# Three-block fp32 kernel on Trainium2: two heads or four matrices in one inverse chain, with shared reciprocal roots

## The chip, the cores and the metric

The kernel runs on one core of one Trainium2 chip. The metric is the time of one execution on the device, in microseconds (us). The engines are TensorE (PE in the profile; PEld is its weight load), VectorE (DVE), ScalarE (ACT), GpSimd (POOL) and SyncE (SP), which issues the DMAs. Each engine executes its instructions in the order in which they were written into its queue.

## The reference

The reference runs three layers, one after the other, on x of 1 x 256 x 2048, all in fp32. The first has two kinds of heads, eight of each. The gated delta rule (GDN) heads need the inverse of a unit triangular matrix, the stick-breaking (SB) heads do not:

```python
# first layer, GDN heads (q, k after a causal convolution, SiLU and L2 norm)
lower = jnp.where(tri_strict, jnp.einsum('nbhik,nbhjk->nbhij', k_beta, k) * decay, 0.0)
t_inv = lax.linalg.triangular_solve(eye + lower, jnp.broadcast_to(eye, lower.shape),
                                    left_side=True, lower=True)
u = t_inv @ v_beta
w = t_inv @ (k_beta * jnp.exp(g)[..., None])
...
# first layer, SB heads (q, k after an RMS norm)
z = jnp.einsum('bhqd,bhkd->bhqk', q_blk, kh) * scale
log_stay = jnp.where(mask, jax.nn.log_sigmoid(-z), 0.0)
between = lax.cumsum(log_stay, axis=3, reverse=True) - log_stay
a = jnp.where(mask, jnp.exp(jax.nn.log_sigmoid(z) + between), 0.0)
...
# second layer, RWKV heads, run forward and backward in time
def step(S, inp):
    r_t, d_t, k_t, v_t, kk_t, b_t = inp
    sa = jnp.einsum('bhij,bhj->bhi', S, -kk_t)
    S = S * d_t[:, :, None, :] + sa[..., None] * b_t[:, :, None, :] + v_t[..., None] * k_t[:, :, None, :]
    return S, jnp.einsum('bhij,bhj->bhi', S, r_t)
```

The rest of the three layers is large projections and feed-forward products. The kernel does the second layer's scan in chunks of 128 rows, which again needs triangular inverses.

## The kernel before

All 256 rows are kept on the chip and the weights stream through it. A panel of weights comes by DMA into one of three slots (`wraw`); ScalarE casts it to its rounded part `whi` (L290), VectorE subtracts to get the rest `wlo` (L291), and TensorE multiplies the split rows with both (L309/L313, L335/L339, L369/L370/L374). A queue of `ada` steps (L496, a 128x2048 multiply with an accumulated sum, which makes the first layer's modulation) is spread over VectorE between the heads by `ada_some`.

Block 1 (to 1440 us) begins with a phase that loads x and the memory and projects the first rows (`project_rows`, to about 205 us). `block1_mix` then runs a loop of nine turns (about 205 to 600 us): GDN head h (`gdn_head`), SB head h-1 (`sb_head`), and the gate and split of GDN head h. Then come the output projection and the feed-forward part. Block 2 runs from about 1470 us with six calls of `rwkv_pair` (two heads, two directions, two chunks of 128 rows each), block 3 from about 2390 us.

`gdn_head` makes three convolved projections, the sums of squares and a reciprocal root on VectorE (`rsqrt`, 11 small operations, L399 to L413), the matrix `gnt` (L781), then calls `pair_inverse`. `rwkv_gram` makes the masked products (`gram`) of one chunk for two heads and calls `pair_inverse` for these two; so each `rwkv_pair` has two chains, one for each chunk. `pair_inverse` doubles the size of the inverted blocks six times. It keeps both the lower (`ylo`) and the upper, transposed inverse (`yup`). Level 0 puts single elements under a mask into both; a level l >= 1 is

- a product of the matrix and `ylo` (L1349),
- copies of `yup` to `z` and of the product to `t` on ScalarE (L1351, L1352),
- the two products `t` with `z` and `z` with `t` (L1358, L1359),
- masked puts of both results into `ylo` and `yup` on VectorE (L1339, `copy_predicated`).

The order on each engine is written by a scheduler that takes the program's order as priority and fills in other work where an instruction is not ready by its own reckoning; so the panels' products stand between the steps of the inverse. Buffers of a tag rotate (`tmp`, lanes A, B and S; two PSUM banks a lane for small products, two for `acc`). The level mask `lev` (128x896, loaded as 448 KB in fp32 and cast on VectorE at L242) is loaded once in the early phase and kept.

## Time and profile before

| | |
|---|---|
| runs, us | 3605.9, 3600.6, 3599.87 (median 3600.6) |
| profiled execution, us | 3601.28, its span 3599.5 |
| mean granted TensorE clock | 0.993 of full |
| busy: TensorE / VectorE / ScalarE / GpSimd | 3514.4 / 2662.4 / 1814.2 / 61.6 us |
| moved by DMA | 700.99 MB, mean 195 GB/s |

Busy times are shares of one span and say nothing of which engine waits for which. Matmul ends in the profile are modelled, so that a TensorE that is marked busy may be between two products. The granted clock is 1.00 at 2.4 GHz and 0.50 at 1.2 GHz; a figure between is a mean over a stretch that had both. The rows that matter stand in the section after the change.

### The profile page before, as it was taken

Reading aid. Unit: us, or ns where it says so; the run is one execution under the profiler, and the core shown is the slowest. Engines: PE = TensorE matmul, PEld = TensorE weight load, DVE = VectorE, ACT = ScalarE, POOL = GpSimd, SP = SyncE. Lnnn points to the kernel's source line nnn. Section 1 sums busy time; section 2 is a strip of 40 time slices with the busy share of each in tenths; the row PEclk is TensorE's granted clock in tenths of the full one; section 3 lists DMA queues with packets and bytes.
Section 4 is the critical chain, followed back from the end, with each engine's and each line's share of the span. In section 5 each row is a group of like instructions: output and inputs, shape, how many; then the busy total and the mean of one; then the engine's idle time right before and its main releaser. Section 6 shows DMA issues by size and latency. Waiting matters only on the chain.

```text
span 3599.5 us, 59008 instructions
## 1 busy us (share of the span) xinstructions
PE 3514.4 (98%) x22656; PEld 3144.6 (87%) x22656; DVE 2662.4 (74%) x5500; ACT 1814.2 (50%) x3138; POOL 61.6 (2%) x190
## 2 busy tenths in 40 slices
PE   8889999999999999999999999999999999999998
PEld 6889998999999998888888888889888888888887
DVE  7788988776767668877878867778776666666666
ACT  4156665544545455555555545554444544444444
POOL 0000000000000000000000000000000000000000
PEclk9989999999999999999999999999999999999999
DMA  8965777656666557332234336574445545555554
GB/s 337 351 237 200 263 266 265 225 208 219 222 206 231 188 181 239 133 125 107 103 115 138 125 117 213 188 253 170 172 168 185 187 176 202 176 198 180 195 184 144
DMA packets 128011, 700.99 MB, mean 195 GB/s; under 512 B 14449, under 2 KB 39537, under 8 KB 58865
## 3 DMA queue, kind: packets, MB, share of 16 engines
q1 hardware_dynamic: 127730, 697.22, 55.0%
q8 instruction: 179, 2.93, 0.3%
q14 instruction: 102, 0.84, 0.1%
HBM read 686.94 MB, written 10.22 MB: 194 GB/s over the span
## 4 chain that ended last, share of the span: by engine, by line
PE 86%; DVE 8%; ACT 3%; DMA 1%; issue 1%; SPq 0%; ACTq 0%; DVEq 0%
PE acc L335 36%; PE acc L339 18%; PE acc L309 12%; PE acc L313 6%; DVE wlo L291 2%; DVE ada L496 2%; PE acc L1349 1%; ACT whi L290 1%; PE acc L1358 1%; PE acc L1359 1%; PE acc L623 1%; PE acc L990 1%; PE acc L374 1%; DMA ada<-in_w_ada 1%; PE acc L369 1%
## 5 line engine op out<-in xcount | busy, mean ns | idle before, releaser
L290 ACT CAST whi<-wraw 128x1024 fp32r<-128x1024 f32 x1118 | 1096.1, 982 | 1199.0 <-PE acc L335 706.9
L291 DVE TENSOR_TENSOR wlo<-wraw,whi 128x1024 fp32r<-128x1024 f32 x1118 | 1272.7, 1140 | 514.5 <-ACT whi L290 412.4
L335 PE MATMUL acc<-a,whi 128*128 128x512 f32 x5888 | 1535.6, 396 | 6.7 <-ACT gt L346 1.7
L335 PEld LDWEIGHTS acc<-a,whi 128*128 128x128 f32 x5888 | 1043.1, 188 | 197.9 <-issue 5.4
L339 PEld LDWEIGHTS acc<-a,wlo 128*128 128x128 f32 x5888 | 816.9, 188 | 75.4 <-issue 4.0
L339 PE MATMUL acc<-a,wlo 128*128 128x256 f32 x5888 | 848.7, 282 | 0.0
L309 PE MATMUL acc<-a,whi 128*128 128x258 f32 (+1 forms) x3872 | 523.5, 284 | 0.2 <-ACT whi L290 0.2
L309 PEld LDWEIGHTS acc<-a,whi 128*128 128x128 f32 x3872 | 485.4, 190 | 0.9 <-ACT whi L290 0.4
L313 PE MATMUL acc<-a,wlo 128*128 128x258 f32 (+1 forms) x1936 | 282.8, 284 | 0.0
L313 PEld LDWEIGHTS acc<-a,wlo 128*128 128x128 f32 x1936 | 252.2, 190 | 0.3 <-issue 0.3
L496 DVE SCALAR_TENSOR_TENSOR ada<-ada,csilu 128x2048 f32<-128x2048 f32 x96 | 219.4, 2285 | 9.0 <-DMA ada<-in_w_ada 8.7
L1339 DVE COPY_PREDICATED ylo<-m_lev,acc 128x128 f32<-128x128 uint8 x200 | 82.8, 416 | 48.6 <-PE acc L1359 47.6
L369 PE MATMUL acc<-whi,a 128*128 128x256 f32 x416 | 108.3, 290 | 1.8 <-ACT whi L290 1.8
L1351 ACT COPY z<-yup 128x128 f32<-128x128 f32 x192 | 56.1, 300 | 102.5 <-DVE yup L1339 59.9
L370 PE MATMUL acc<-whi,a 128*128 128x256 f32 x416 | 107.6, 288 | 0.0
L356 DVE TENSOR_TENSOR x<-acc,x 128x256 f32<-128x256 f32 x128 | 54.2, 424 | 51.7 <-PE acc L339 51.7
L347 DVE TENSOR_TENSOR gt<-acc,gt 128x256 f32<-128x256 f32 x214 | 89.0, 418 | 3.5 <-ACT gt L346 2.9
L346 ACT COPY gt<-acc 128x256 f32<-128x256 f32 x214 | 78.0, 364 | 17.6 <-PE acc L339 17.6
L369 PEld LDWEIGHTS acc<-whi,a 128*128 128x128 f32 x416 | 80.0, 192 | 2.8 <-ACT whi L290 2.0
L370 PEld LDWEIGHTS acc<-whi,a 128*128 128x128 f32 x416 | 79.9, 192 | 0.0
L1359 PE MATMUL acc<-z,t 128*128 128x128 f32 x384 | 72.4, 278 | 0.2 <-ACT t L1352 0.2
L1358 PE MATMUL acc<-t,z 128*128 128x128 f32 x336 | 69.2, 290 | 2.0 <-ACT t L1352 2.0
(514 smaller groups left out, 3372.7 us busy)
## 6 DMA issues: line engine op xcount, KB each, us to landing
wraw<-in_w_up SPq DMA_DIRECT2D x132, 1024.0 KB, 4.8
ada<-in_w_ada SPq DMA_DIRECT2D x96, 1024.0 KB, 5.2
wraw<-in_w_down SPq DMA_DIRECT2D x128, 704.0 KB, 4.1
wraw<-in_w_out SPq DMA_DIRECT2D x48, 1024.0 KB, 4.9
wraw<-in_w_mg SPq DMA_DIRECT2D x48, 1024.0 KB, 4.9
wraw<-in_w_gate SPq DMA_DIRECT2D x44, 1024.0 KB, 4.7
wraw<-in_w_rs SPq DMA_DIRECT2D x20, 1024.0 KB, 5.1
wrow<-in_w_rows SPq DMA_DIRECT2D x16, 1024.0 KB, 8.5
```

Of the source, the lines that this page charges most:

```text
L290: nc.scalar.copy(hi[:, :m], raw[:, a:a + m])
L291: nc.vector.tensor_sub(lo[:, :m], raw[:, a:a + m], hi[:, :m].bitcast(F32))
L309: nc.tensor.matmul(acc, w, m, start=(n == 0), stop=False)
L313: nc.tensor.matmul(acc, lo[:, k % 8 * P:k % 8 * P + P], hs[k - c * kt][0], start=False, stop=(n == last))
L335: nc.tensor.matmul(both, hi[:, k % 8 * P:k % 8 * P + P], hs[k - c * kt][2], start=(n == 0), stop=False)
L339: nc.tensor.matmul(acc[:, :T], lo[:, k % 8 * P:k % 8 * P + P], hs[k - c * kt][0], start=False, stop=(n == last))
L347: self.nc.vector.tensor_add(out, acc[0], out)
L369: self.nc.tensor.matmul(accs[t], hs[k][0][:, ts], hi[:, ws], start=(k == 0), stop=False)
L370: self.nc.tensor.matmul(accs[t], hs[k][1][:, ts], hi[:, ws], start=False, stop=False)
L496: nc.vector.scalar_tensor_tensor(raw, raw, 1.0, self.cs, op0=ALU.mult, op1=ALU.mult, accum_out=self.mod[:, n:n + 1])
L1358: nc.tensor.matmul(pu4[:, 0, h], z2[:, h], t1[:, h], start=True, stop=True)
L1359: nc.tensor.matmul(pu4[:, 1, h], t1[:, h], z2[:, h], start=True, stop=True)
```

## The change

`gdn_head` becomes `gdn_pair`: the convolutions of two heads (lanes A and B), one reciprocal root for the eight columns of both, the preparation of both (`gdn_prep`), one `group_inverse` for the two matrices, both scans (`gdn_scan`), one reciprocal root for the four output columns. `sb_head` becomes `sb_pair`: the projections of two SB heads, one root of eight columns, then the two attends (`sb_attend`). The loop of `block1_mix` has five turns. In block 2, `rwkv_gram` no longer inverts: both chunks write into one tile `grams` (matrices of 128x512 in all), cleared by one memset on GpSimd, and one `group_inverse` takes the four matrices. In `group_inverse` a level makes all lower products and one put of all, then all upper products and one put of all. The level mask is loaded twice, in block 1's pool with two casts and in block 2's with four. In all, VectorE has 4969 instructions where it had 5406, ScalarE 2900 for 3092, GpSimd 156 for 194, TensorE 21043 as before.

```diff
-                self.load_mask(self.const, "lev")
...
+        self.lev2 = self.load_levels(bp, 2)
...
-        for h in range(9):
-            if h < 8:
-                with self.on("AB"[h % 2]):
-                    o = self.gdn_head(h)
-            if h:
-                self.sb_head(h - 1, ob)
-            if h < 8:
-                oa[h] = self.gdn_out(h, o, self.z_gate(h))
+        for i in range(5):
+            if i < 4:
+                pair = self.gdn_pair(2 * i)
+            if i:
+                self.sb_pair(2 * i - 2, ob)
+            if i < 4:
+                for h, o in enumerate(pair):
+                    oa[2 * i + h] = self.gdn_out(2 * i + h, o, self.z_gate(2 * i + h))
...
+    def gdn_pair(self, h0):
...
+        for j, lane in lanes:
+            with self.on(lane):
+                k = self.conv_proj("w1_k", h0 + j, 8 + h0 + j, "gk")
+                q = self.conv_proj("w1_q", h0 + j, h0 + j, "gq")
+                self.sumsq_cols(k, ss, 4 * j)
+                self.sumsq_cols(q, ss, 4 * j + 2)
+                kqv.append((k, q, self.conv_proj("w1_v", h0 + j, 16 + h0 + j, "gv")))
+        with self.on("A"):
+            nc.vector.tensor_scalar(sse, ss[:, :8], 1e-6, None, op0=ALU.add)
+            self.rsqrt(r, sse, [P, 8], "g")
+        preps = []
+        for j, lane in lanes:
+            with self.on(lane):
+                preps.append(self.gdn_prep(h0 + j, *kqv[j], r[:, 4 * j:4 * j + 4], sse[:, 4 * j:4 * j + 4], nt[:, j]))
+        lo, up = self.group_inverse(nt, self.lev2, "AB", lower=True)
+        outs = []
+        for j, lane in lanes:
+            with self.on(lane):
+                outs.append(self.gdn_scan(kqv[j][0], preps[j], [up[:, 1, j], lo[:, 1, j]]))
...
+    def sb_pair(self, h0, ob):
...
+        self.rsqrt(rk, mk, [P, 8], "s")
+        for j in range(2):
+            hv = slice(j * P, j * P + P)
+            self.sb_attend(h0 + j, *qk[j], rk[:, 4 * j:4 * j + 4], sv[0][:, hv], sv[1][:, hv], ob)
...
+        grams = self.bp.tile([P, 7, 4, P], F32, name=self.uid("gram"), tag="gram", bufs=1)
+        nc.gpsimd.memset(grams, 0.0)
         for n in range(2):
             with self.on("AB"[n]):
-                g, up = self.rwkv_gram(n, preps)
-                grams.append(g)
-                ups.append(up)
+                self.rwkv_gram(n, preps, grams)
+        _, up = self.group_inverse(grams[:, 0], self.lev4, "AB")
...
-        for h in range(H):
-            put(up, h, 0, mats[h])
-            put(lo, h, 0, pn[:, h * P:h * P + P])
+        put(up, 0, one(mats))
+        put(lo, 0, pn)
         for l in range(1, 7):
...
+            pt = bank(lanes[1])
+            for h, hc in enumerate(heads):
+                nc.tensor.matmul(flat(pt[:, hc], l), mats[:, h], zipped(lo, l, h, 1), start=True, stop=True)
+            nc.scalar.copy(flat(one(z2), l), zipped(up, l))
+            nc.scalar.copy(one(t1), pt)
             both = l < 6 or lower
+            pl = bank(lanes[0]) if both else None
+            if both:
+                for h, hc in enumerate(heads):
+                    nc.tensor.matmul(pl[:, hc], z2[:, h], t1[:, h], start=True, stop=True)
+                put(lo, l, pl)
+            pu = bank(lanes[1])
+            for h, hc in enumerate(heads):
+                nc.tensor.matmul(pu[:, hc], t1[:, h], z2[:, h], start=True, stop=True)
+            put(up, l, pu)
```

Where the order moves, three places. First VectorE at the start of block 1's heads, from the first sums of squares (`gss`) to the first puts of level 1; `ada` is a step of the modulation, `gnt` the matrix to be inverted, the last figures are the shape of the output. Before:

```order
L743 TENSOR_SCALAR gss_1465<-acc_1456 128x4
...
L779 SCALAR_TENSOR_TENSOR gdec_1492<-acc_1506,gnlam_1483,gdec_1492 128x128 x2
...
L781 TENSOR_TENSOR gnt_1511<-gdec_1492 128x128
...
L1339 COPY_PREDICATED yup_1528<-m_lev,gnt_1511 128x64x2
L1339 COPY_PREDICATED ylo_1527<-m_lev,acc_1533 128x64x2
...
L1339 COPY_PREDICATED ylo_1527<-m_lev,acc_1541 128x32x2x2
L1339 COPY_PREDICATED yup_1528<-m_lev,acc_1541 128x32x2x2
```

and now, from the first `ada` step behind a row copy on:

```order
L496 SCALAR_TENSOR_TENSOR ada_1783,mod<-ada_1783,csilu 128x2048
...
L1357 CAST m_lev_1403<-mraw_1404 128x7x128
...
L1357 CAST m_lev_1403<-mraw_1404 128x7x128
...
L748 TENSOR_SCALAR gss_1434<-acc_1433 128x8
...
L496 SCALAR_TENSOR_TENSOR ada_1852,mod<-ada_1852,csilu 128x2048
...
L821 SCALAR_TENSOR_TENSOR gdec_1529<-acc_1543,gnlam_1520,gdec_1529 128x128 x2
...
L822 TENSOR_TENSOR gnt_1436<-gdec_1529 128x128
L821 SCALAR_TENSOR_TENSOR gdec_1575<-acc_1589,gnlam_1566,gdec_1575 128x128 x2
...
L822 TENSOR_TENSOR gnt_1436<-gdec_1575 128x128
...
L1379 COPY_PREDICATED yup_1610<-m_lev_1403,gnt_1436 128x128x2
L1379 COPY_PREDICATED ylo_1609<-m_lev_1403,acc_1615 128x128x2
```

Both matrices `gnt` stand ahead of the first put (L1379), and two `ada` steps and the two casts of the mask have come ahead of it.

Second TensorE at the end of block 1's heads. L883/L917 spread the roots, L891/L925 make the scores, L906/L940 begin the sums over the softplus `ssp`, L915/L947 the output of an SB head; only products of the output panels stand in the places left out, and in the first gap before also the last GDN head. Before:

```order
L891 MATMUL acc_5967<-sq_q_5873,sq_k_5937 128x128 x3
...
L906 MATMUL acc_5980<-ssp_5972,c_negtri 128x128
...
L915 MATMUL acc_5987<-sz_5971,sv_5801 128x128
...
L883 MATMUL acc_6214<-c_ident,srk_6200 128x128 x2
L891 MATMUL acc_6218<-sq_q_6124,sq_k_6188 128x128 x3
...
L906 MATMUL acc_6231<-ssp_6223,c_negtri 128x128
...
L915 MATMUL acc_6238<-sz_6222,sv_5801 128x128
```

and now:

```order
L925 MATMUL acc_5829<-sq_q_5600,sq_k_5664 128x128 x3
...
L940 MATMUL acc_5842<-ssp_5834,c_negtri 128x128
...
L947 MATMUL acc_5849<-sz_5833,sv_5527 128x128
...
L917 MATMUL acc_5855<-c_ident,srk_5811 128x128 x2
L925 MATMUL acc_5859<-sq_q_5736,sq_k_5800 128x128 x3
...
L940 MATMUL acc_5872<-ssp_5864,c_negtri 128x128
...
L947 MATMUL acc_5879<-sz_5863,sv_5527 128x128
```

The scores of the last head now follow directly on the output of the one before it; 15 panel products (3.48 us of TensorE by the order's sizes at 0.23 us for 512 columns) stand between the scores and the sums of the first of the two heads, 4 (0.92 us) in the second.

Third TensorE inside an inverse of block 2: `gram` is the matrix, L1349/L1390 open a level, L335/L339 are products of the panels. Before (two chains, of buffers `ylo_20178` and `ylo_20301`):

```order
L335 MATMUL acc_20502<-a_15656,whi_20498 128x512
L1358 MATMUL acc_20227<-t_3520_20180,z_3521_20181 128x128
L1359 MATMUL acc_20227<-z_3521_20181,t_3520_20180 128x128
...
L1349 MATMUL acc_20314<-ylo_20301,gram_20279 128x128
...
L1349 MATMUL acc_20236<-ylo_20178,gram_20154 128x128
L1358 MATMUL acc_20320<-t_3543_20303,z_3544_20304 128x128
L1349 MATMUL acc_20236<-ylo_20178,gram_20156 128x128
L1359 MATMUL acc_20320<-z_3544_20304,t_3543_20303 128x128
...
L1358 MATMUL acc_20242<-t_3520_20180,z_3521_20181 128x128
...
L1349 MATMUL acc_20329<-ylo_20301,gram_20277 128x128
```

and now, from the last transpose on:

```order
L1384 MATMUL acc_19601<-c_ident,gram_19553 128x128
...
L335 MATMUL acc_19818<-a_15309,whi_19814 128x512
L1390 MATMUL acc_19608<-ylo_19595,gram_19553 128x128 x4
L335 MATMUL acc_19818<-a_15312,whi_19814 128x512
...
L1397 MATMUL acc_19615<-t_3383_19597,z_3384_19598 128x128 x4
L1401 MATMUL acc_19621<-z_3384_19598,t_3383_19597 128x128 x4
L1390 MATMUL acc_19627<-ylo_19595,gram_19553 128x128 x4
L339 MATMUL acc_19818<-a_15300,wlo_19815 128x256
...
L1397 MATMUL acc_19634<-t_3383_19597,z_3384_19598 128x128 x4
```

Four products stand together at each step of one chain, where the steps of two chains of two alternated.

## Rows read from the trace of the kernel before

**Rows 1.** The page's first part: busy us (share of the span) and instructions of each engine.

```profile
PE 3514.4 (98%) x22656; PEld 3144.6 (87%) x22656; DVE 2662.4 (74%) x5500; ACT 1814.2 (50%) x3138; POOL 61.6 (2%) x190
```

**Rows 2.** Busy time by stretch: us, each engine (instructions), granted clock, DMA share, GB/s.

```profile
205.00:240.00 35.00, 30.86 (x196) 28.26 (x196) 28.93 (x92) 22.80 (x54) 2.75 (x7) 0.80 0.49 161
...
260.00:575.00 315.00, 304.02 (x2452) 292.30 (x2451) 283.85 (x722) 197.86 (x450) 13.76 (x18) 0.99 0.70 249
575.00:605.00 30.00, 23.42 (x133) 19.24 (x132) 23.98 (x67) 20.39 (x47) 0.00 (x0) 0.94 0.55 200
...
1470.00:2140.00 670.00, 657.44 (x4095) 554.18 (x4094) 533.22 (x1499) 354.65 (x798) 32.13 (x78) 1.00 0.33 114
```

**Rows 3.** Groups by line, TensorE, 260-575 us: count | busy, mean | idle before.

```profile
L1358 PE MATMUL acc<-t,z 128*128 128x128 f32 x84 | 18.6, 303 | 1.6 <-ACT t L1352 1.6
L1349 PE MATMUL acc<-ylo,gnt 128*128 128x128 f32 x84 | 18.0, 295 | 3.4 <-DVE ylo L1339 1.1 <-DVE rs L400 1.0 <-ACT go L841 0.6
...
L1342 PE MATMUL acc<-c_ident,gnt 128*128 128x128 f32 x7 | 2.0, 292 | 1.8 <-DVE gnt L781 1.8
```

**Rows 4.** The same view of TensorE, block 2's heads, 1470 to 2140 us.

```profile
L1349 PE MATMUL acc<-ylo,gram 128*128 128x128 f32 x288 | 59.5, 296 | 4.1 <-DVE ylo L1339 2.3 <-DVE rs L400 0.4 <-DVE rq L401 0.4
...
L1342 PE MATMUL acc<-c_ident,gram 128*128 128x128 f32 x24 | 6.1, 283 | 3.3 <-DVE gram L1272 3.0 <-DVE rs L399 0.2
```

**Rows 5.** Timeline, TensorE, start of block 1: start us, duration us, instructions [idle before].

```profile
207.57 1.11 PE L313 MATMUL acc<-a,wlo 128*128 128x256 f32 x8
208.52 2.04 PE L309 MATMUL acc<-a,whi 128*128 128x256 f32 x16
...
236.43 0.48 PE L1349 MATMUL acc<-ylo,gnt 128*128 128x128 f32 x2 [0.22 <-DVE rs L400]
```

**Rows 6.** Groups by line, VectorE (and the last row ScalarE), whole span.

```profile
L291 DVE TENSOR_TENSOR wlo<-wraw,whi 128x1024 fp32r<-128x1024 f32 x974 | 1190.0, 1223 | 427.3 <-ACT whi L290 412.4 <-ACT gt L346 5.1 <-ACT t L1352 4.5
L496 DVE SCALAR_TENSOR_TENSOR ada<-ada,csilu 128x2048 f32<-128x2048 f32 x96 | 219.4, 2285 | 9.0 <-DMA ada<-in_w_ada 8.7
...
L1339 DVE COPY_PREDICATED yup<-m_lev,acc 128x128 f32<-128x128 uint8 x192 | 61.3, 326 | 2.7 <-PE acc L1359 2.6
...
L1272 DVE COPY_PREDICATED gram<-m_tri_b,acc 128x256 f32<-128x256 uint8 x48 | 19.0, 441 | 1.5 <-PE acc L1267 1.5
...
L649 DVE SCALAR_TENSOR_TENSOR gk<-row,half_conv_qkv,gk 128x256 f32<-128x256 f32 x15 | 7.2, 477 | 0.2 <-ACT gk L647 0.2
...
L1468 ACT COPY sm<-acc 128x512 f32<-128x512 f32 x16 | 9.4, 585 | 8.7 <-PE acc L1466 8.6
```

**Rows 7.** Timeline, VectorE, early phase and start of block 1.

```profile
81.98 0.62 DVE L242 CAST m_lev<-mraw 128x896 uint8<-128x896 f32 x1
...
222.35 0.16 DVE L743 TENSOR_SCALAR gss<-acc 128x4 f32<-128x4 f32 x1 [2.12 <-PE acc L729]
...
234.37 0.73 DVE L1339 COPY_PREDICATED yup<-m_lev,gnt 128x128 f32<-128x128 uint8 x1
```

**Rows 8.** Timeline, TensorE and ScalarE, end of block 1's heads.

```profile
569.95 0.83 PE L891 MATMUL acc<-sq_q,sq_k 128*128 128x128 f32 x6
...
576.37 0.49 PE L906 MATMUL acc<-ssp,c_negtri 128*128 128x128 f32 x2
...
579.97 0.49 PE L915 MATMUL acc<-sz,sv 128*128 128x128 f32 x2 [1.11 <-ACT sz L911]
...
585.54 1.04 PE L891 MATMUL acc<-sq_q,sq_k 128*128 128x128 f32 x6 [0.57 <-DVE sq_q L884]
...
588.00 0.36 ACT L898 ACTIVATE sz<-acc,srk 128x128 f32<-128x128 f32 x1
...
589.49 1.28 ACT L901 ACT_TABLE_LOAD   x1
```

**Rows 9.** Timeline, VectorE, first level of an inverse in block 2.

```profile
1503.24 0.93 DVE L1339 COPY_PREDICATED yup<-m_lev,gram 128x128 f32<-128x128 uint8 x1
...
1503.80 0.95 DVE L1339 COPY_PREDICATED ylo<-m_lev,acc 128x128 f32<-128x128 uint8 x1
```

More of the change, by code (lines that the diff above doesn't have):

```diff
@@ L1253, in rwkv_rates, with rwkv_gram @@
         return ar, bk, kd, carry
-    def rwkv_gram(self, n, dirs):
+    def rwkv_gram(self, n, dirs, grams):
         nc, c = self.nc, self.c
         ch = slice(n * P, n * P + P)
-        grams = []
-        for h in range(2):
-            g = self.tmp("gram", (P, 7, P), bufs=2)
-            nc.gpsimd.memset(g, 0.0)
-            grams.append(g)
         for d, (ar, bk, _, _) in enumerate(dirs):
@@ L1268, in rwkv_gram @@
             mask = c["tri_b" if d else "tri_f"].rearrange("p (a t) -> p a t", a=2)
-            for g, pg in zip(grams, pgs):
+            for h, pg in enumerate(pgs):
+                g = grams[:, :, 2 * n + h]
                 for j in range(2):
@@ L1280, in rwkv_scan @@
         first, second = (1, 0) if d else (0, 1)
-        g = {(n, h, j): grams[n][h][:, j + 3 * d] for n in range(2) for h in range(2) for j in (1, 2, 3)}
-        ys = [[up[:, h, 1 - d] for h in range(2)] for up in ups]
+        g = {(n, h, j): grams[:, j + 3 * d, 2 * n + h] for n in range(2) for h in range(2) for j in (1, 2, 3)}
+        ys = [[up[:, 1 - d, 2 * n + h] for h in range(2)] for n in range(2)]
         state = None
@@ L1322, in rwkv_scan, with load_levels @@
                     nc.scalar.activation(state[hs, hs], pS[hs, hs], AF.Copy, scale=carry[hs])
-    def pair_inverse(self, mats, lower=False):
+    def load_levels(self, pool, copies):
+        lo, w = CCOL["lev"]
+        t = pool.tile([P, 7, copies, P], U8, name=f"m_lev{copies}")
+        f = self.wp.tile([P, 2048], F32, name=self.uid("mraw"), tag="wraw", bufs=WRAW)
+        self.nc.sync.dma_start(f[:, :w], self.ins["consts"][:, lo:lo + w])
+        f3 = f[:, :w].rearrange("p (l t) -> p l t", l=7)
+        for j in range(copies):
+            self.nc.vector.tensor_copy(t[:, :, j], f3)
+        return t.rearrange("p l h t -> p l (h t)")
@@ L1325, in pair_inverse, with group_inverse @@
+    def group_inverse(self, mats, lev, lanes, lower=False):
         nc = self.nc
-        H = len(mats)
-        lev = self.c["lev"].rearrange("p (l t) -> p l t", l=7)
-        lo, up = (self.tmp(n, (P, H, 2, P)) for n in ("ylo", "yup"))
-        t1, z2 = self.tmp("t1", (P, H, P)), self.tmp("z2", (P, H, P))
+        H = mats.shape[1]
+        with self.on(lanes[0]):
+            lo, up = (self.tmp(n, (P, 2, H, P)) for n in ("ylo", "yup"))
+            t1, z2 = self.tmp("t1", (P, H, P)), self.tmp("z2", (P, H, P))
@@ new lines, in zipped, with bank @@
+        def zipped(t, l, h=0, n=H):
+            v, s = t[:, 0, h], 1 << l
+            return bass.AP(v.tensor, v.offset, [v.ap[0], (2 * s, n * 64 // s), (H * P + s, 2), (1, s)])
+        def bank(lane):
+            with self.on(lane):
+                return self.psum(False)[:, :H * P]
+        flat = lambda ap, l: ap.rearrange("p (m e s) -> p m e s", e=2, s=1 << l)
+        put = lambda t, l, src: nc.vector.copy_predicated(zipped(t, l), flat(lev[:, l], l), flat(src, l))
+        heads = [slice(h * P, h * P + P) for h in range(H)]
```

162 lines of the change are left out of this document (74 added, 88 removed).

## The prediction

> **What bounds the kernel now.** I read the busy shares first: TensorE 98% of the span, VectorE 74%, ScalarE 50% [rows 1]. The change leaves every matrix product in place (21043 TensorE instructions in the order before and after), so no TensorE work goes away. What can change is TensorE's idle time and its granted clock in the two stretches that the edit touches. The table of stretches tells how much there is [rows 2]. In block 1's heads (205 to 605 us) TensorE is busy 30.86 of 35 us at the start at clock 0.80, and 304.02 of 315 in the middle; the last 30 us hold 23.42. Block 2 holds 657.44 of 670. The idle time is thus some 4 + 11 + 7 us in these block 1 stretches and 12.6 in block 2. That sum, 35 us or 1% of the span, is the most that this edit could give back, apart from clock. VectorE is busy 283.85 of 315 us in the middle of block 1: a relief there can count, and a late VectorE is felt at once.
>
> The idle time must lie at the inverse for the edit to win it. In the middle of block 1 the rows give 3.4 us before the product that opens a level (L1349), 1.6 before L1358 and 1.8 before the transposes, 6.8 in all over 7 chains [rows 3]. In block 2 it is 4.1 and 3.3 over 12 chains [rows 4]. These figures are low: a lone 128x128 record lasts 0.295 us and the end is modelled, while in an unbroken run a 256-column record starts 0.95/8 = 0.12 us after the last one [rows 5]; so every wait can hide up to 0.17 us more as "busy".
>
> **The change, part by part.** The sum is made against the profiled execution, 3601.28 us, 0.7 above the median of 3600.6. About 0.2%, 7 us, is what a measurement of this kernel can tell from no change.
>
> *Middle of block 1: -7 us.* Eight chains of six levels become four. Each level keeps its products, but they come in groups of two, so the waits per level stay and the levels halve. Half of the 6.8 us seen is 3.4. With the hidden part (7 chains x 6 levels x 2 waits x at most 0.17 = 14 us, halved 7) it is 10.4. VectorE also drops 12 of 24 reciprocal-root chains, 12 to 14 tiny operations of 0.16 us each (as L743 in [rows 7]), some 2 us a chain and 24 us in all; that is worth nothing by itself, yet it shortens the queue ahead of the puts (an ada step of 2.285 us stands between two puts of one chain more than once). I take 7, ends 3 and 10.
>
> *Start of block 1: +5 us.* The first shared inverse needs both heads' preparation, and VectorE runs in order. By the order printed above it now also executes, ahead of the first put, two ada steps (2.285 each, [rows 6], as all durations of this sentence but the casts), two mask casts (0.62 each, by the one of the same size before [rows 7]), the second head's preparation (some 2 us: four to six steps of this size) and seven convolution steps of a third head (0.48 long, begun some 0.4 apart: 2.8), and two fewer weight residues (1.22 each: -2.4): some 8 us more. Before, the first put stood at 234.37 us, and VectorE had idled 2.12 us for one product ahead of it [rows 7] and smaller gaps besides, which the new work can fill. So the put moves by 2 to 8 us; I take 4. In that time TensorE has less to do: 104 panel products of 256 columns stand ahead of the first level instead of 121, 17 x 0.12 = 2 us, less 0.7 for the second head's own products that come early. 4 + 1.3 is 5; ends 1 and 11, the upper one with 2 us for a longer stay at the low clock (the granted clock there is 0.80, a mix of the two levels, [rows 2]).
>
> *End of block 1: +6 us.* Before, the attends of heads 6 and 7 were a head apart, and only the last stood bare. Now they follow each other at the very end, and TensorE takes the second one's scores after the first one's output. From the scores' end to the next product an attend took 576.37 - 570.78 = 5.6 us, with the load of an activation table (1.28) in it; ScalarE's part alone, from the first function at 588.00 to the table's end at 590.77 and one more function of 0.5, is 3.3 us, and with VectorE's two steps of about 0.6 some 4.5 [rows 8]. The order leaves 3.48 us of panel work in the first and 0.92 in the second. So idle: 1.0 to 2.1 and 3.6 to 4.7 us in these two places, 0.57 before the scores and 1.1 before the output (the waits of [rows 8]) twice: 8 to 10. Before, those of one attend and one more output wait stood there, 0.57 + 1.1 + 1.1 = 2.8. The difference is 5 to 7; the low clock after a gap may add a little. I take 6, ends 4 and 9.
>
> *Block 2: 0 us.* One chain of four matrices replaces two that filled each other's waits. For: 72 chain levels become 36, and the 4.1 us before L1349 with up to 72 x 2 x 0.17/2 = 12 hidden could halve, -8, and VectorE and ScalarE have fewer fixed costs. Against: all four matrices must be ready before level 0 is put, and a put is now 512 wide. At level 0 the 128-wide puts started 0.56 us apart [rows 9]. No row has a 512-wide one; if the cost is by element it is 4 x 0.56 = 2.2, if it has a fixed part of a tiny operation (0.16) it is 1.8. I take 2.1, nearer the row itself. Two puts (upper and lower) then stand between the last gram copy and the first level: 4.2, and with the last gram copies (0.44 each, [rows 6]) 5.5 us, where the order holds 2.6 us of other TensorE work: 2.9 bare, six times, 17 us, against some 5 to 7 before (3.3 seen [rows 4] and the hidden part). That is +10, and -10 for the levels (-8, and 2 for fewer waits at the scans): 0; ends -10 and +13. Inside a level TensorE has 12 products of two records each, 0.11 us apart (six records took 0.83 us, [rows 8]), 2.7 us, and the loop (products 0.9, copy 0.585, products 0.9, put 0.8 by 0.16 + 4 x (0.326 - 0.16), [rows 6]) is 3.2, with 0.5 to 1 us of other work in the order: covered. Level 1, with pairs two apart, is the tightest.
>
> Here a rule of the Trainium skill would price the level-0 put otherwise. The page "Vector Engine (DVE) Microarchitecture Reference", section "Measured stream behaviour on trn2", gives some 75 ns an instruction and 1.04 ns a column, and 1.7 ns where one port hops at every element. By it (an estimate from that page) the 512-wide put is about 0.95 us. The rows disagree with it for the 128-wide one, which by it would be 0.29 us, where they show 0.56. By the rows the sum is +4, by the page -9.
>
> *Masks: 0.* One 448 KB load leaves the early phase, which is bound by transfers (about 1 us), and four casts of some 0.62 us come at the start of block 2. Ends -1 and +2. What moves with the buffers is hidden: the wider POOL fills stand a whole pair ahead of their use.
>
> Sum: -7 + 5 + 6 + 0 + 0 = +4, so 3601.28 + 4 = 3605 us: **no change that can be measured**.
>
> **Rivals.** *Slower, by the start.* The decisive place is the first level-1 product of the first pair. It stood at 236.43 us before [rows 5]. In the forecast it comes near 240.5; each us later is a us of the kernel, since by the order TensorE's panel work ahead of it is spent. The threshold of 7 us is passed from 244 on, the rest unchanged. For it: TensorE waits there for VectorE and ScalarE alone, and the clock was low already (0.80). Against: VectorE had some 6 of 35 us idle in that stretch [rows 2]. With the put 8 us later and 2 us of clock the start costs 11, and the sum is +10: 3611. The bare last attend works to the same side.
>
> *Faster, by the levels.* The middle gives 10 instead of 7, block 2's levels give -8 net, the start costs 3: -10 + 3 + 6 - 8 = -9, 3592. For it: VectorE at 90% in the middle, so its relief shortens many queues. Against: only 11 us of idle are there to be won [rows 2].
>
> *Faster, by a cheap level-0 put.* If a put's cost per element falls with width, the 4.2 us of the two puts become about 1.9; the bare 2.9 us per pair shrinks to 0.6, 6 x 2.3 = 14, and -13 with the rest gives +4 - 13 = -9, 3592. The two puts' rows speak against it: 0.56 us for 128 columns. The page named above would have it so.
>
> **How the numbers follow.** The forecast has 0.40, the slower rival 0.32 (the start alone, or start and end together near their upper ends), the levels 0.20, the cheap put 0.08. Faster by over 0.2%: 0.28; within: 0.40; slower: 0.32. The range runs from the faster cases with a little more (3601 - 16) to start and block 2 near their upper ends (+6 and +13 over the forecast): 3585 to 3625. The same-only range would be 3594 to 3608.
>
> **What would show it.** Right: the idle before the level products of block 1 about half; first level-1 product near 240 us; two gaps of 1 to 5 us on TensorE between scores and the next product at the end; in block 2 one gap of about 3 us per pair ahead of the first level, and VectorE's level-0 put near 2.1 us. Wrong: a first level before 237 us or after 244; a level-0 put near 1 us; gaps inside levels 2 to 6 of block 2 of over 0.5 us, which would mean that one chain can't be covered; block 1's middle with the same idle as before, which would mean that the inverse was never its cause.

## The result and the profile after

The changed kernel takes 3651.17 us (median of four runs, 3649.16 to 3652.19), the one before in the same session 3600.23: a ratio of 1.0144, 95% interval 1.0132 to 1.0156. It is **51 us slower**. The forecast was 3605, in a range from 3585 to 3625.

The page's first part, to be read against [rows 1]:

```profile
PE 3531.1 (97%) x22656; PEld 3158.9 (87%) x22656; DVE 2657.3 (73%) x5063; ACT 1784.5 (49%) x2946; POOL 52.6 (1%) x152
```

VectorE has 437 instructions fewer and only 5 us less busy time. TensorE has the same instructions and is busy 17 us longer.

For what follows the span is cut at five events: the last product of the row phase, the first product of level 1, the last output product of the SB heads, the first gram product of block 2 and its last scan product. Busy time by these stretches (columns as in [rows 2]), before:

```profile
205.50:236.40 30.90, 26.78 (x165) 24.32 (x164) 24.83 (x81) 21.00 (x49) 2.75 (x7) 0.78 0.55 181
236.40:596.40 360.00, 342.93 (x2701) 326.82 (x2701) 322.35 (x814) 225.72 (x509) 14.48 (x19) 0.99 0.70 248
596.40:1493.20 896.80, 891.63 (x6417) 839.55 (x6415) 647.58 (x1095) 457.57 (x668) 10.87 (x64) 1.00 0.62 213
1493.20:2107.30 614.10, 603.31 (x3788) 508.26 (x3787) 487.40 (x1372) 325.26 (x746) 32.13 (x78) 1.00 0.32 110
```

and after:

```profile
200.90:238.80 37.90, 28.51 (x153) 25.47 (x152) 33.77 (x98) 23.64 (x55) 1.50 (x5) 0.73 0.55 190
238.80:607.90 369.10, 344.76 (x2713) 330.17 (x2714) 309.45 (x595) 215.88 (x454) 8.70 (x13) 0.97 0.69 244
607.90:1512.00 904.10, 896.39 (x6419) 843.36 (x6417) 652.21 (x1097) 457.04 (x668) 11.25 (x59) 1.00 0.61 211
1512.00:2155.90 643.90, 613.29 (x3800) 515.79 (x3799) 484.61 (x1143) 304.54 (x608) 29.74 (x53) 0.98 0.31 106
```

The start costs 7.0 us, the heads 9.1, the stretch to block 2 7.3, block 2 29.8; the row phase ended 4.6 earlier in this execution. Block 2 is the largest, and splits in two: TensorE's idle time goes from 10.8 to 30.6 us (+19.8), its busy time rises by 10.0 for the same products. Where the idle time lies, by groups of TensorE's lines from 1488 to 2190 us (L1390 opens a level, as L1349 in [rows 4]):

```profile
L1390 PE MATMUL acc<-ylo,gram 128*128 128x128 f32 x288 | 46.2, 307 | 20.6 <-DVE ylo L1379 17.6 <-DVE sm L1503 3.0
L1397 PE MATMUL acc<-t,z 128*128 128x128 f32 x240 | 34.9, 290 | 1.3 <-ACT t L1392 1.0
L1505 PE MATMUL acc<-c_ident,sm 128*128 128x128 f32 x64 | 12.2, 300 | 3.4 <-DVE sm L1503 3.4
L1384 PE MATMUL acc<-c_ident,gram 128*128 128x128 f32 x24 | 7.3, 304 | 3.5 <-DVE gram L1300 3.3 <-DVE rs L399 0.2
```

The 4.1 us ahead of L1349 have become 20.6 ahead of L1390. 17.3 of them stand at one place, once in each of six pairs (2.64 to 3.05 us; the one of 3.05 is put down to `sm`, a step of a softmax that stood in VectorE's queue there). TensorE's and then VectorE's timeline at the entry of the third inverse:

```profile
1773.88 1.32 PE L335 MATMUL acc<-a,whi 128*128 128x512 f32 x5
1778.10 1.90 PE L1390 MATMUL acc<-ylo,gram 128*128 128x128 f32 x8 [2.89 <-DVE ylo L1379]
...
1783.94 1.16 PE L1390 MATMUL acc<-ylo,gram 128*128 128x128 f32 x8 [0.48 <-DVE ylo L1379]
```

```profile
1773.41 2.43 DVE L1379 COPY_PREDICATED yup<-m_lev,gram 128x512 f32<-128x512 uint8 x1
1775.45 2.59 DVE L1379 COPY_PREDICATED ylo<-m_lev,acc 128x512 f32<-128x512 uint8 x1
1777.66 1.43 DVE L291 TENSOR_TENSOR wlo<-wraw,whi 128x1024 fp32r<-128x1024 f32 x1
```

Two level-0 puts hold VectorE from 1773.41 to 1778.0, and TensorE runs out of other products at 1775.2. The records of such puts overlap, so their price to VectorE is best read from start to start: 2.04 us for the first, 2.21 for the second. In the kernel before, the puts of one chain of block 2 stood so:

```profile
1849.80 0.73 DVE L1339 COPY_PREDICATED yup<-m_lev,gram 128x128 f32<-128x128 uint8 x1
1850.30 0.79 DVE L1339 COPY_PREDICATED ylo<-m_lev,acc 128x128 f32<-128x128 uint8 x1
1850.71 0.95 DVE L1339 COPY_PREDICATED yup<-m_lev,gram 128x128 f32<-128x128 uint8 x1
1851.27 0.95 DVE L1339 COPY_PREDICATED ylo<-m_lev,acc 128x128 f32<-128x128 uint8 x1
1851.84 1.65 DVE L1272 COPY_PREDICATED gram<-m_tri_f,acc 128x256 f32<-128x256 uint8 x4
```

Four puts of 128 columns held VectorE for 2.04 us, as long as one of 512 does now. The merged put is no slower by the element and hardly cheaper; what is new is that all eight puts' worth of work stands in one piece ahead of the first product. What the gap does to TensorE afterwards shows in the five microseconds before and after the first product of the level (two of the six pairs; the six behave alike, with 0.66 or 0.67 behind the gap):

```profile
1773.10:1778.10 5.00, 2.11 (x14) 1.46 (x12) 5.00 (x5) 0.67 (x1) 0.00 (x0) 1.00 0.01 3
1778.10:1783.10 5.00, 5.00 (x27) 4.71 (x28) 1.49 (x2) 1.63 (x2) 0.00 (x0) 0.66 0.59 200
1886.03:1891.03 5.00, 2.11 (x13) 1.46 (x12) 5.00 (x5) 0.67 (x1) 0.00 (x0) 0.99 0.00 0
1891.03:1896.03 5.00, 5.00 (x27) 4.71 (x28) 1.53 (x2) 1.64 (x2) 0.00 (x0) 0.66 0.62 195
```

A mean of 0.66 is two thirds of the time at 1.2 GHz and one third at 2.4. Five microseconds at 0.66 do the work of 3.3; 1.7 lost in each of six pairs make 10.2 us, the 10.0 by which the busy time of block 2 rose.

### The profile page after: what moved, and what is told of

Same layout as the page of the kernel before. It is cut to its first block, busy times and chain, and to the rows that moved or that the text cites. A ratio compares the mean times of both kernels' runs of the same rounds, so it can differ in the third digit from the quotient of the medians.

```text
span 3649.1 us, 58199 instructions
## 1 busy us (share of the span) xinstructions
PE 3531.1 (97%) x22656; PEld 3158.9 (87%) x22656; DVE 2657.3 (73%) x5063; ACT 1784.5 (49%) x2946; POOL 52.6 (1%) x152
## 4 chain that ended last, share of the span: by engine, by line
PE 84%; DVE 10%; ACT 3%; issue 2%; DMA 1%; SPq 0%; ACTq 0%; DVEq 0%
PE acc L335 36%; PE acc L339 18%; PE acc L309 12%; PE acc L313 6%; DVE wlo L291 2%; DVE ada L496 2%; PE acc L1390 1%; ACT whi L290 1%; PE acc L1397 1%; PE acc L1401 1%; DVE ylo L1379 1%; PE acc L1022 1%; PE acc L622 1%; PE acc L369 1%; PE acc L370 1%
## 5 line engine op out<-in xcount | busy, mean ns | idle before, releaser
L335 PE MATMUL acc<-a,whi 128*128 128x512 f32 x5888 | 1539.4, 397 | 7.2 <-DVE a L391 2.7
L335 PEld LDWEIGHTS acc<-a,whi 128*128 128x128 f32 x5888 | 1045.9, 188 | 204.5 <-DVE a L391 6.4
L339 PEld LDWEIGHTS acc<-a,wlo 128*128 128x128 f32 x5888 | 818.2, 189 | 74.4 <-issue 0.7
L339 PE MATMUL acc<-a,wlo 128*128 128x256 f32 x5888 | 842.9, 282 | 0.0
L309 PE MATMUL acc<-a,whi 128*128 128x258 f32 (+1 forms) x3872 | 525.1, 286 | 2.8 <-ACT whi L290 2.8
L309 PEld LDWEIGHTS acc<-a,whi 128*128 128x128 f32 x3872 | 490.2, 191 | 4.7 <-ACT whi L290 3.5
L1391 ACT COPY z<-yup 128x512 f32<-128x512 f32 (+1 forms) x60 | 32.4, 541 | 103.0 <-DVE yup L1379 92.4
L1379 DVE COPY_PREDICATED ylo<-m_lev,acc 128x512 f32<-128x512 uint8 (+1 forms) x64 | 58.4, 913 | 30.3 <-PE acc L1397 30.0
L374 PE MATMUL acc<-wlo,a 128*128 128x256 f32 x416 | 68.8, 283 | 0.0
L1390 PE MATMUL acc<-ylo,gram 128*128 128x128 f32 x288 | 46.2, 307 | 20.6 <-DVE ylo L1379 17.6
```

Source lines behind the costliest of these rows:

```text
L309: nc.tensor.matmul(acc, w, m, start=(n == 0), stop=False)
L335: nc.tensor.matmul(both, hi[:, k % 8 * P:k % 8 * P + P], hs[k - c * kt][2], start=(n == 0), stop=False)
L339: nc.tensor.matmul(acc[:, :T], lo[:, k % 8 * P:k % 8 * P + P], hs[k - c * kt][0], start=False, stop=(n == last))
L1379: put = lambda t, l, src: nc.vector.copy_predicated(zipped(t, l), flat(lev[:, l], l), flat(src, l))
L1390: nc.tensor.matmul(flat(pt[:, hc], l), mats[:, h], zipped(lo, l, h, 1), start=True, stop=True)
```

## The experiments

**Which half.** The changed block 1 with block 2 as before (`a1_block1_only`), and the reverse (`a2_block2_only`).

```diff
# a1: block 2 as before
...
-        _, up = self.group_inverse(grams[:, 0], self.lev4, "AB")
...
+                g, up = self.rwkv_gram(n, preps)     # calls pair_inverse for each chunk
...
# a2: block 1 as before
-        for i in range(5):
+        for h in range(9):
...
```

> The change in block 1 alone; block 2's inverses are those of the kernel before, its level mask loaded there once. Theory (the loss is two separate losses, block 1 some 11 us net of a 4.6 us shorter early phase, block 2 some 30 with its masks): 3609 to 3616 us. Rival (the paired heads of block 1 cost little and the loss in block 2 is all there is): 3597 to 3604 us. Rival (the two parts disturb one another, through buffers or the order): neither this run nor the next adds up to 3651.

> The change in block 2 alone; block 1 and the early load of the mask are those of the kernel before. Theory: block 2's one chain costs 28 us and its four mask casts 2 to 4, so 3628 to 3635 us, and the gains over the kernel before of this run and the last one add up to 51 us within 4. In its trace TensorE stands idle 2.9 us ahead of the first level of each pair and the granted clock falls to the lower level right behind it.

Measured: 3623.7 us (1.0065, 1.005 to 1.008) and 3630.65 us (1.0083, 1.0068 to 1.0098). Over the kernel before in their session, 3599.97, that is 23.7 and 30.7, together 54 for 51: the halves add up, and each has a loss of its own. Block 2's is as expected, and the trace of a2 shows the same six gaps (2.64 to 3.05 us). Block 1's is larger than any of its ranges. Of the 22.4 us that a1's trace has over the one before, start and heads hold 14.7 and the stretch to block 2, where a late mask load stands, 4.3; block 2 and what follows, whose inverses and products are those of before, hold 5.3, and the row phase ended 1.9 earlier.

**The entry of block 2's inverse.** Four edits of the changed kernel and two of the one before. First the order of the two puts; the level needs only the lower one.

```diff
-        put(up, 0, one(mats))
         put(lo, 0, pn)
+        put(up, 0, one(mats))
```

> The changed kernel, with the two puts of level 0 exchanged: the lower one first, which is all that the first product of level 1 needs. Theory (the entry of the chain is the loss: two 512-wide level-0 puts of 2.44 us in series): the first level starts 2.4 us earlier, some of it comes back as a wait for the upper half at the copy to z, and the clock holds up better, 1.6 to 3 us a pair: 3632 to 3641 us. Rival (the loss is that one chain has no second one to fill its levels): 3647 to 3652 us.

Measured: 3651.8 us (1.0142, 1.0127 to 1.0158), no gain: a time in the rival's range, though c2 below refutes the rival's reason. TensorE's groups in block 2:

```profile
L1390 PE MATMUL acc<-ylo,gram 128*128 128x128 f32 x288 | 43.0, 292 | 11.7 <-DVE ylo L1379 8.6 <-DVE sm L1503 3.0
L1397 PE MATMUL acc<-t,z 128*128 128x128 f32 x240 | 34.0, 285 | 8.0 <-ACT t L1392 7.8
L1505 PE MATMUL acc<-c_ident,sm 128*128 128x128 f32 x64 | 12.2, 293 | 7.7 <-DVE sm L1503 7.7
```

The wait moved: 9 us less ahead of L1390, 6.7 more behind ScalarE's copies (which need the upper put) and 4.3 more for the softmax `sm` queued behind both. VectorE's 4.6 us are the price, whoever stands behind them.

Next, level 0 put chunk by chunk, so that chunk 0's put overlaps chunk 1's gram products (`a4_level0_by_chunk`), and the kernel before with its two chains kept and only the puts of two matrices grouped (`a5_chunk_chains`).

```diff
# a4
...
+        for first, count, ready in parts or [(0, H, None)]:
...
+            for t, src in ((up, one(mats)), (lo, pn)):
+                nc.vector.copy_predicated(zipped(t, 0, first, count), flat(lev[:, 0, sl], 0), flat(src[:, sl], 0))
# a5, in before
-        _, up = self.pair_inverse([g[:, 0] for g in grams])
+        _, up = self.group_inverse(grams[:, 0], self.lev2, self.lane * 2)
```

> The changed kernel, with level 0 of block 2's chain done in two halves: the two matrices of chunk 0 are put (256 wide) while chunk 1's gram products still run; levels 1 to 6 as in the change, one chain of four. Theory (entry): only 2 x 1.3 us stand between the last gram copy and the first level, so the 2.9 us of idle time fall below 1 and the clock stays up: 3 to 4 us a pair, 3627 to 3634 us. Rival (one chain can't be covered inside its levels): 3644 us or more.

> The kernel before, with block 2 kept as two chains (one per chunk), each with the changed inverse for its two matrices: one 256-wide put instead of two of 128, all lower products before all upper ones. It parts the two things that the change did to block 2. Theory (the loss is that all four matrices enter at once; grouping puts is itself a small gain): block 2's heads take 605 to 615 us where they took 614, and 3592 to 3602 us in all with two late mask casts. Rival (the grouped order inside a level, the upper products after the lower put, is what costs): 625 us or more in block 2, 3612 us or more.

Measured: 3636.17 us (1.0098, 1.0081 to 1.0115), block 2 626.7 us instead of 643.9 in its trace, the slowest of four runs; and 3612.14 us (1.0037, 1.0022 to 1.0052), block 2 620.5. Both missed to the slow side, a5 with the time of its rival. In a5 not one matrix more waits than before, and still L1403, which opens a level there, waits 11.6 us for 4.1, 9.3 of them for `ylo`. So the joint start of four matrices isn't needed for a loss. That a grouped level-0 put is enough (two records of 1.3 us or more, where a first product waited for two puts of 128 before) is argued from these waits and not shown: a5 also has the grouped order inside its levels and a late mask load.

That left the put itself. Level 0 writes at every element from one half of the tile to the other. The next kernel (`c1_level0_in_rows`) computes the same by a masked copy of all 1024 elements in a row (512 in block 1), with a mask that takes odd columns in one half and even ones in the other: twice the elements, and no change of half at every element.

```diff
-        put(up, 0, one(mats))
-        put(lo, 0, pn)
+        first = self.first.unsqueeze(2).to_broadcast([P, 2, H, P])
+        for t, src in ((up, mats), (lo, pn.rearrange("p (h t) -> p h t", h=H))):
+            nc.vector.copy_predicated(t, first, src.unsqueeze(1).to_broadcast([P, 2, H, P]))
```

> The changed kernel, with level 0 put another way: one masked copy over whole rows of both halves (1024 contiguous elements for four matrices), in place of 512 elements that jump between the halves at every element. The same values are written. Theory (the two 2.44 us puts keep VectorE, and all that stands behind them, for 4.9 us a pair): a put takes 1.1 to 1.4 us, 2.1 to 2.6 us less a pair, the idle time ahead of the first level falls from 2.9 below 1 us and the clock holds: 3630 to 3638 us. Rival (waiting for all four matrices is what costs, however they are put): 3645 us or more.

Measured: 3620.05 us (1.0056, 1.0039 to 1.0073), 31 us faster than the changed kernel and better than expected. VectorE's puts of level 0 in block 2, TensorE's opening product, and block 2 as a whole:

```profile
L1391 DVE COPY_PREDICATED yup<-m_first,gram 128x1024 f32<-128x1024 uint8 x6 | 8.1, 1344 | 0.0
L1391 DVE COPY_PREDICATED ylo<-m_first,acc 128x1024 f32<-128x1024 uint8 x6 | 7.9, 1321 | 0.0
```

```profile
L1395 PE MATMUL acc<-ylo,gram 128*128 128x128 f32 x288 | 41.7, 287 | 3.2 <-DVE ylo L1383 3.2
```

```profile
1514.20:2128.40 614.20, 603.41 (x3803) 508.95 (x3802) 467.36 (x1143) 305.02 (x609) 29.50 (x53) 1.00 0.33 111
```

Against the changed kernel's

```profile
L1379 DVE COPY_PREDICATED yup<-m_lev,gram 128x512 f32<-128x512 uint8 x6 | 14.7, 2446 | 0.0
```

a little over half the time for twice the elements. Idle (10.8), busy (603.4) and clock (1.00) are all those of the kernel before: these two puts, with the clock behind them, were the whole of block 2's loss. With it chunk by chunk too, and block 1 as before (`c2_block2_mended`):

```diff
+            mask = self.first.unsqueeze(2).to_broadcast([P, 2, count, P])
+            for t, src in ((up, mats), (lo, pn.rearrange("p (h t) -> p h t", h=H))):
+                nc.vector.copy_predicated(t[:, :, hs], mask, src[:, hs].unsqueeze(1).to_broadcast([P, 2, count, P]))
```

> The change in block 2 alone, with both mends: level 0 by whole rows, and chunk 0's two matrices put while chunk 1's gram products run. Theory: with the entry near that of the kernel before and the levels 10 us cheaper (as the run with level 0 by chunk showed), block 2's heads take 604 to 614 us where the kernel before took 614 and the change alone 642; with the mask casts 3594 to 3604 us in all. Rival (a single chain of four has a loss besides its level 0): 3612 us or more.

Measured: 3598.61 us (1.0001, 0.9992 to 1.001), as expected. One chain for four matrices is worth nothing measurable once its entry is mended.

Last, how much of the loss was the clock alone: the changed kernel with 24 transposes more in the gap, whose results nobody reads (`d1_spare_products`).

```diff
+        if H == 4:
+            for _ in range(6):
+                spare = bank(lanes[1])
+                for h, hc in enumerate(heads):
+                    nc.tensor.transpose(spare[:, hc], mats[:, h], self.ident)
```

> The changed kernel, with 24 more transposes of the four gram matrices a pair, into banks that nothing reads, ahead of the first level of block 2: 2.7 us of TensorE work in the gap of 2.9 us. They add nothing to the result. Theory (a gap costs its own length and then the lower clock behind it, some 1.7 us a pair): the gap is filled, the granted clock stays at 1.00 behind it, and the kernel is 6 to 11 us faster though it does more: 3640 to 3645 us. Rival (the clock behind the gap costs nothing of its own, other waits cover it): 3650 to 3655 us.

Measured: 3666.03 us (1.0191, 1.0175 to 1.0206), a miss by over 20 us. The clock held behind the opening product at five of the six entries, as at the third here:

```profile
1783.01:1788.01 5.00, 3.10 (x28) 2.76 (x26) 4.85 (x3) 0.67 (x1) 0.00 (x0) 1.00 0.00 0
1788.01:1793.01 5.00, 4.67 (x35) 4.19 (x36) 2.99 (x3) 0.59 (x1) 0.00 (x0) 1.00 0.15 23
...
2012.47:2017.47 5.00, 3.10 (x27) 2.76 (x26) 4.86 (x3) 0.67 (x1) 0.00 (x0) 1.00 0.01 3
2017.47:2022.47 5.00, 5.00 (x29) 5.00 (x30) 2.22 (x2) 0.59 (x1) 0.00 (x0) 0.66 0.19 26
```

The last two lines are the exception, the fifth entry: the same idle time ahead (1.90 of 5 us), and the clock fell. And at the first entry it fell too, only earlier: a wait of 2.95 us for `sm` stood among the spare products there, with 0.66 in the five microseconds ahead of the opening product.

But the products did not fit into the gap, which the opening product still shows, and more VectorE work came late behind it:

```profile
L1395 PE MATMUL acc<-ylo,gram 128*128 128x128 f32 x288 | 42.0, 288 | 11.5 <-DVE ylo L1379 9.5 <-DVE den L1504 1.9
...
L1510 PE MATMUL acc<-c_ident,sm 128*128 128x128 f32 x64 | 11.4, 294 | 13.9 <-DVE sm L1508 13.9
```

10.5 us more than in the changed kernel wait for `sm`. That the clock falls because of the gap is shown by this run and c1 together: shorter gaps here spare four of the six entries, and c1, without the gap, has 1.00 in the five microseconds before and after all six opening products. That the clock's 10 us could be had back alone is not shown.

**Block 1.** These four have block 2 as before. SB heads one by one (`b1_single_sb`), one root for each GDN head (`b2_root_per_head`), a lighter start (`b3_light_start`: the mask cast in the early phase, and the gates of heads 0 and 1 without the `ada` step of VectorE that each draws), and b1 with b3 (`b4_single_sb_light_start`).

```diff
# b1
-                self.sb_pair(2 * i - 2, ob)
+                self.sb_head(2 * i - 2, ob)
+                self.sb_head(2 * i - 1, ob)
...
# b2
+                self.rsqrt(r[:, cols], sse[:, cols], [P, 4], "g")    # per head
...
# b3
+                self.lev2 = self.load_levels(self.const, 2)    # early phase
...
-        acc = self.proj("w1_z", h)
+        acc = self.proj("w1_z", h) if h > 1 else self.ftile(self.ins["w1_z"][h], self.hs)    # proj with no ada step
```

> The change in block 1 alone (3623.7 us), with the stick-breaking heads single again, one after the other, each with its own root; the gated-delta heads stay paired. Theory (of block 1's loss, the bare last attend is some 5.5 us and the waits for the shared roots 2.6): 3613 to 3618 us. Rival (the loss is all in the paired gated-delta heads): 3621 to 3625 us.

> The change in block 1 alone, with one reciprocal root per gated-delta head in place of the shared one, the rest as it was (11 more tiny operations a pair on VectorE). If waiting for the second head's sums of squares is what costs, this is 3617 to 3621 us; if sharing the roots is of no matter for TensorE, it stays within 3621 to 3626 us, which is what I expect.

> The change in block 1 alone, with VectorE relieved at the start: the level mask and its two casts in the early phase, and no step of the modulation with the first two gate projections. Theory (the start loses 6 to 7 us because VectorE does these 6.8 us ahead of the first put): from the last row product to the first level 31 to 33 us instead of 37, and 3617 to 3620 us. Rival (the start is bound by the second head's preparation itself): 36 us or more, 3621 us or more.

> The change in block 1 alone, with single stick-breaking heads and the light start together. Theory (start 3 and end 5 us, independent of one another): 3614 to 3618 us, so some 15 of the 24 us are left for the paired gated-delta heads and for the masks. Rival (the waits only move from one to the next): 3619 to 3623 us.

Measured, against a1's 3623.7: b1 3620.34 (1.0057, 1.0042 to 1.0072), b2 3626.22 (1.0076, 1.0061 to 1.0091), b3 3620.31 (1.0061, 1.0044 to 1.0077), b4 3619.73 (1.0057, 1.0042 to 1.0072). Start and heads together took 405.6 us in a1's trace, 400.2 in b1's, 400.4 in b3's, 398.8 in b4's and 390.9 before. The end of the SB pair and the heavy start are each worth some 5 us in the traces and 3 in the medians, which is within the intervals, but not both together: b1 and b4 missed their ranges to the slow side, b4 into that of its rival, by which the waits only move. Sharing the roots is worth nothing that shows.

Two more kernels asked for the rest: everything mended (`e1_all_mends`: c2's block 2, b4's block 1, level 0 in rows in both), and the same with one chain for each head of block 1 (`e2_two_chains`).

```diff
# e2 against e1
-        lo, up = self.group_inverse(nt, self.lev2, "AB", lower=True)
+                inv.append(self.group_inverse(nt[:, j:j + 1], self.lev2[:, :, :P], lane * 2, lower=True))
```

> The changed kernel with every mend found so far: level 0 as one masked copy of contiguous rows in both blocks, block 2's level 0 chunk by chunk, SB heads one by one, the mask for two cast in the early phase and the z panels of the first two heads by another path. Theory A (what is left of block 1's loss is the one shared chain of two heads: both preparations must be done before any level, and one chain has no second to fill its waits): block 1's heads from the end of the rows to the last output take 396 to 399 us (390.9 before, 398.8 in the run with single SB heads and a light start), block 2 615 to 617, the time 3605 to 3611. Theory B (what is left comes of the two heads' projections, preparations and scans standing side by side, whoever inverts): the same here. Theory C (block 1's loss was the hopping level-0 copy too, as in block 2): block 1 at 391 to 393 and the time 3598 to 3602.

> As the run with all mends, but the two heads of block 1 are inverted by two chains of one matrix each, on the two lanes, as before the change; all else in pairs. Theory A (the shared chain): block 1's heads 4 to 6 us shorter than in the run with all mends, the time 3600 to 3605. Theory B (the bunched preparations and scans): block 1 within 2 us of the run with all mends, or longer by up to 4 for the fixed costs of more puts; the time within 3605 to 3613.

Measured: 3609.29 us (1.0029, 1.0019 to 1.004) and 3611.2 us (1.0036, 1.0023 to 1.0049). Start and heads of e1:

```profile
202.90:234.70 31.80, 23.33 (x161) 20.86 (x159) 26.57 (x93) 21.87 (x53) 1.50 (x5) 0.90 0.40 135
234.70:592.80 358.10, 341.54 (x2706) 329.07 (x2706) 311.34 (x641) 216.45 (x454) 8.12 (x13) 0.97 0.71 252
```

389.9 us in sum, less than theory C's 391 and near the 390.9 before; e2's are 396.2. So the shared chain was not at fault (two chains are no better). By this trace start, SB pairs and level-0 put would account for block 1, but other numbers do not agree. The time, 3609.29, is that of theories A and B. Unpaired heads took 386.9 us in c2's trace and 387.9 in a5's. The level-0 put in rows alone took 2.7 off start and heads in c1 (404.3 for 407.0). And the median of e1 is still 11 us over c2, which differs from it in block 1 and its mask alone. The profiled execution of e1 (3605.8) was its fastest of nine. Over c2 its trace has 3.0 us in start and heads, 2.5 up to block 2 and 4.2 behind block 2, where the code is the same. That last stretch took from 1487.5 to 1497.2 us over the traces cut in this way, so a difference of a few us in one stretch of one trace can't be put down to an edit. What the last 11 us of the paired block 1 are stays **open**. No version beats the kernel before; c2 equals it.

## Why the prediction was wrong, point by point

*Block 2: 0 us, it was +30.* This is the step that failed. Its price for the entry was right: from start to start the two puts held VectorE for 4.25 us, where 4.2 were worked out (2.04 and 2.21 for 2.1 each), and TensorE stood bare for 2.89 us where I had 2.9. A level's put took 0.83 us on the mean for the 0.8 taken. What failed is, first, the **"-10 for the levels"** set against the gap. Nothing of it is seen: outside of the six gaps the opening products still wait 3.3 us (20.6 less 17.3) for 4.1, and in c1, with the clock at 1.00, TensorE is as busy as before (603.4 us for 603.3), so no wait was hidden in its records that fewer levels gave back. Second, what I took off the gap as waits that would go, "some 5 to 7 before": 3.3 us of it are those ahead of the transposes, and they stayed (L1384, 3.5). So the idle time ahead of the opening products rose by 16.5 where 10 were priced. Third, what stood in no term: **the clock behind the gap**. I priced a longer stay at the low clock at block 1's start and not in block 2, where each of six gaps brought 5 us at 0.66: 10 us. The in-order queue behind the two puts is a fourth cost without a term: small here (L1505 waits 3.4 us where its like waited 2.5), but 4.3 of the 9 us that a3 won went there.

The signs that I had named for "right" in block 2 both came, one gap of about 3 us a pair and a put near 2.1 us, and the block was still 30 us slower. They tested the costs that I had counted, and neither the gain set against them nor the clock.

c1 and c2, with puts of a little over half the length, come out even (614.2 and 615.9 us for 614.1). That is the balance that I forecast, but not the reason: neither a cost nor a gain shows in c1's idle time.

The rule of the Trainium skill that made one rival (the page "Vector Engine (DVE) Microarchitecture Reference", section "Measured stream behaviour on trn2": 1.7 ns an element where one port hops, measured on another operation) gave 0.95 us for this put, as an estimate. The trace disagrees: 2.04 and 2.21 us from start to start, 4.0 to 4.3 ns an element. The spacing of the 128-wide puts, 0.56 us, was the better guide.

*Start of block 1: +5, it was +7.* Within its ends of 1 and 11. The first level came at 238.80 for the 240.5 forecast, but the rows had ended 4.6 us sooner in that execution; from the rows' end it is 37.9 us for 30.9. TensorE waited on the way for a weight residue queued behind the two mask casts, 1.08 us each where I took 0.62, for `gkdec`, and for a residue behind an `ada` step; then for the puts:

```profile
206.73 1.22 PE L313 MATMUL acc<-a,wlo 128*128 128x256 f32 x8 [2.78 <-DVE wlo L291]
...
220.15 0.68 PE L819 MATMUL acc<-gk 128*128 128x128 f32 x4 [1.91 <-DVE gkdec L810]
...
229.44 2.08 PE L313 MATMUL acc<-a,wlo 128*128 128x256 f32 x8 [2.29 <-DVE wlo L291]
...
238.80 0.72 PE L1390 MATMUL acc<-ylo,gnt 128*128 128x128 f32 x4 [1.44 <-DVE ylo L1379]
```

*End of block 1: +6, it was about that.* b1 gives 5.4 us back in the trace, 3.4 in the median. The gaps stand where [rows 8] had one set of them:

```profile
591.46 0.46 PE L940 MATMUL acc<-ssp,c_negtri 128*128 128x128 f32 x2 [1.37 <-DVE ssp L936]
593.99 0.80 PE L947 MATMUL acc<-sz,sv 128*128 128x128 f32 x2 [1.40 <-ACT sz L945]
597.16 1.62 PE L925 MATMUL acc<-sq_q,sq_k 128*128 128x128 f32 x6 [0.67 <-DVE sq_q L918]
603.57 0.46 PE L940 MATMUL acc<-ssp,c_negtri 128*128 128x128 f32 x2 [3.09 <-DVE ssp L936]
606.71 0.79 PE L947 MATMUL acc<-sz,sv 128*128 128x128 f32 x2 [1.61 <-ACT sz L945]
```

Together 8.1 us, for the 8 to 10 worked out, of which 2.8 had stood there before.

*Middle of block 1: -7, it was a loss of some 3.* Failed too. The 6.8 us that I saw at the inverse, over seven matrices, became 3.9 over six. The gain lies at the transposes (L1384, which no longer wait for 1.8); the level products L1390 and L1397 wait 0.65 us a matrix for 0.71, so they did not halve. And waits came where there were none, at the panels, at the roots and at the scores. TensorE's groups from 265 to 590 us:

```profile
L1397 PE MATMUL acc<-t,z 128*128 128x128 f32 x72 | 12.3, 293 | 0.7 <-ACT t L1392 0.7
L1390 PE MATMUL acc<-ylo,gnt 128*128 128x128 f32 x72 | 11.8, 287 | 3.2 <-DVE ylo L1379 2.1 <-DVE rs L412 1.1
L309 PE MATMUL acc<-a,whi 128*128 128x256 f32 x976 | 142.6, 290 | 2.1 <-ACT whi L290 2.1
L917 PE MATMUL acc<-c_ident,srk 128*128 128x128 f32 x28 | 4.5, 285 | 2.3 <-DVE srk L401 2.3
L825 PE MATMUL acc<-gq,gk 128*128 128x128 f32 x24 | 4.4, 314 | 2.2 <-DVE gkdec L810 2.2
L1384 PE MATMUL acc<-c_ident,gnt 128*128 128x128 f32 x6 | 1.8, 301 | 0.0
```

The like of L309, L917 and L825 had no wait from 260 to 575 us before. Of the hidden 7 us, worked out as a bound from records' lengths, I booked half as a gain; nothing of it was seen. With the clock at 0.97 for 0.99 the heads as a whole were 9.1 us longer, of which the end is some 6.

*Masks: 0, the stretch that holds them is 7 longer.* The casts are 1.08 us for 0.62, which explains 2 of it at most. a1, with one cast for block 2 in place of four, has 901.1 us there, and c2, with the four, 900.9. Each trace with a late mask load that was cut in this way has 900.9 to 907.2 us there, where the one before has 896.8; what of this is the masks' can't be told from one trace of each.

*The rivals.* "Slower by the start" named a true loss and the wrong main one. The cheap put did not come: the two took 4.25 us, where it had 1.9. No rival had block 2 lose more than 13, though I had its gap right: its bill ended at the gap.

## What to carry to other kernels

Merging several small copies into one saves little where the elements set the time and not the count: here one put of 512 columns held VectorE as long as four of 128. The pattern of access was the price, a copy that changes halves at every element being slower than a contiguous one of twice the elements, and the mend was to copy more. Merged work also holds an in-order engine in one piece; price the gap it leaves on the other engine, then the clock behind that gap, and then whoever is queued behind the piece. And a gain inferred from what a modelled record may hide should not be set against a cost that is counted.

## What the runs showed of the hardware

- A masked copy on VectorE into elements that alternate between two halves took 2.45 us for 512 elements a partition and 1.32 for 256 by its record; in rows, 1.34 us for 1024 (1.3 ns an element for 4.8). From start to start it is 2.04 and 2.21 us for 512, and 2.04 for four of 128; in rows 1.23 and 1.20 for 1024 (c1, third pair). At levels 1 to 6, where the runs are longer, a 512-wide put took 0.83 on the mean, 1.3 at level 1.
- A cast of 128x896 to 8 bits took 1.08 us into a tile that holds two or four copies side by side; the one before, into a plain tile, took 0.62 [rows 7]. The copies side by side are not the reason by themselves: in c1, casts of six of the seven levels (128x768) into the same kinds of tile took 0.55. What the seventh level changes stays open.
- Gaps of 2.64 to 3.05 us on TensorE were each followed by 5 us at a mean granted clock of 0.66 or 0.67, at all six entries. With spare products in the gap (d1) 1.90 to 1.94 us of idle time were followed by 1.00 at four entries and by 0.66 at one.
